# Two of eight low weight parts of a filler job made by an accumulating transfer, and four buffers for the parts

## The chip, the core and the metric

The kernel runs on one core of a Trainium2 chip. The metric is the time of the whole launch on the device, in microseconds. A core has TensorE (PE in the profile; PEld is its weight load), VectorE (DVE), ScalarE (ACT), GpSimd (POOL) and SyncE (SP), each with its own instruction stream, and 16 DMA engines which all of them feed. Here SP issues the loads of the weights, POOL issues small reshuffling transfers and some loads of 256 KB to 512 KB, and ACT issues the stores of results.

## The reference

The reference is one layer of a bidirectional hybrid encoder for a sequence of 256 tokens with 2048 features, in fp32. Cut to what matters here:

```python
mod = silu(c) @ W_ada + b_ada            # shift, scale, gate for mixer and FFN
h = rms_norm(x) * (1 + scale_m) + shift_m
u = h @ W_in                             # q,k,v,o,gates of an mLSTM | q,k,v,z,beta,decay of a gated delta rule | two merge gates
y_a = bidirectional chunkwise mLSTM(u)             @ W_a      # 4 heads
y_b = bidirectional chunkwise gated delta rule(u)  @ W_b      # 16 heads of 128, with a 5-tap convolution
x = x + gate_m * ((g_a * y_a + g_b * y_b) @ W_out)
x = x + gate_f * swiglu(rms_norm(x) * (1 + scale_f) + shift_f)
out = rms_norm(x)
```

The weights of the projections are read once from HBM, and most of TensorE's work is the products of the 256 tokens with them.

## The kernel before

**Products in three parts.** An fp32 product is computed as three products of a shorter type (fp32r in the profile). Each operand is the sum of a high part (the value copied to fp32r) and a low part (the value minus the high part). The result is high times high plus low activation times high weight plus high activation times low weight. The activations are split once (`hh`, `hl` for h). The weights arrive as fp32 and are split on the chip: ScalarE copies a piece of the raw tile to `wh` (line 182 or 213), VectorE subtracts `wh` from the raw piece into `wl` (line 184 or 215).

**Jobs.** A job is one slab of weight columns. `fjob` (line 173) makes 128 columns with the features on the partitions. `tjob` (line 199) makes 512 columns with the tokens on the partitions. The raw weights of a `tjob` come as four chunks `u` of 1 MB, each with four blocks of 128 rows; SP asks for them. Half a chunk, two blocks, is a quantum `(u, k0)` with `k0` 0 or 2, so a job has eight. For each quantum the inner function `halves` (line 207) makes `wh` and `wl`, tiles of 128 x 1024 elements (4 KB for each partition); then come twelve matmuls 128 x 512 (lines 234, 235, 236: high by high, high weight by low activation, low weight by high activation). `wh`, `wl` and the raw tiles are rings of three buffers each; the ring of the raw tiles is shared with the tiles of the modulation weights (`ada`). A part can be written when the matmuls that read the buffer's last content are done.

**Order.** The program is traced in Python as generators that yield after each quantum, and a scheduler may move instructions within what their dependences allow, unless the instruction is wrapped in `order(...)`, which keeps it in program order among the ordered ones of its engine. In `halves` the copy and the subtraction are ordered only where the job makes parts early (`early`). `settle()` runs small pieces of work that were put off; it is called between the copy and the subtraction.

**The delta-rule stage.** From about 131 us to 990 us the kernel computes the delta rule in four groups of four heads: `gdn_phase1` for each head (norms, the products of keys and queries, decays), `gdn_invert` for a group (the inversion of small triangular matrices, VectorE on 64 partitions, with tiles reshuffled by small POOL transfers `inst_d`, `uu`, `inv_d`, `cg`), `gdn_blocks`, and `gdn_phase2` for a pair of heads (chains of small matmuls with VectorE and ScalarE between). These chains leave TensorE time, which filler jobs take: a call of `fill(n)` emits n quanta of the next job. The jobs by token in this stage are z (the delta rule's output gate), v and o (of the mLSTM), mb and ma (the merge gates), four of each; the jobs by feature are the heads' projections `b` and the mLSTM's `a`. VectorE also sums the `ada` tiles in the background (line 111, 128 x 2048).

**After it** come the mLSTM, the branch projections `yb` and `ya`, and the output projection `o` (to about 1240 us), the FFN's gate and up projections `gt`, `up` (to about 1755 us) and its down projection `d`, all with the same `tjob`.

The functions that the diff touches, and what calls them:

Of the kernel before, what the change touches and what calls it, by code (L numbers as in the profile page):

```python
# [10 lines left out]
F32R = mybir.dt.float32r  # L11
AF = mybir.ActivationFunctionType
ALU = mybir.AluOpType
PSUM = bass.MemoryType.PSUM

P = 128
# [36 lines left out]
def hybrid_block(ctx: ExitStack, tc: tile.TileContext, xr, nfr, crow, pk_d, cst_d, ada2, ada4, win0, winb, wint, wba, wbb, wo, wgu, wd, out, dbg=None):  # L53
    nc = tc.nc
    V, S, G, PE = nc.vector, nc.scalar, nc.gpsimd, nc.tensor

    def pool(stack, name, bufs=1, **kw):
        return stack.enter_context(tc.tile_pool(name=name, bufs=bufs, **kw))

    cp = pool(ctx, "cp")  # L60
    st = pool(ctx, "st")
# [9 lines left out]
    def order(ins, yes=True):  # L71

        return tc.keep_in_program_order(ins) if yes else ins
# [62 lines left out]
    def raw_tile(shape, name):  # L136

        since[0] += 1
        if since[0] > 2 and asked and room[0][0] is st:
            add()  # L140
        return st.tile(shape, F32, tag="raw", bufs=3, name=name)
# [4 lines left out]
    def settle(keep=0, only=None):  # L146

        now = [f for f in behind if only is None or f.__name__ == only]
        for f in now[: len(now) - keep]:
            behind.remove(f)  # L150
            f()
# [13 lines left out]
    def pump():  # L165
        count[0] += 1
        if every[0] and count[0] % every[0] == 0:
            owed[0] += 1
        if owed[0] and not held[0]:
            owed[0] -= 1  # L170
            sums()

    def fjob(name, src, done):

        ps = acc_ps.tile([P, 512], F32, tag="acc", name=f"acc_{name}")
        o = ps[:, :T]
        raw = raw_tile([P, KB, P], f"raw_{name}")
        nc.sync.dma_start(raw, src)
        for k0 in range(0, KB, 8):
            wh = st.tile([P, 8, P], F32R, tag="wh", bufs=3, name=f"wh_{name}_{k0}")  # L180
            wl = st.tile([P, 8, P], F32R, tag="wl", bufs=3, name=f"wl_{name}_{k0}")
            S.activation(wh, raw[:, k0 : k0 + 8], AF.Copy)
            settle()
            V.tensor_tensor(wl, raw[:, k0 : k0 + 8], wh.bitcast(F32), ALU.subtract)  # L184
            for k in range(8):
                kk = k0 + k
                PE.matmul(o, wh[:, k], woven(hh[:, kk]), start=kk == 0, stop=False)  # L187
                PE.matmul(o, wh[:, k], woven(hl[:, kk]), start=False, stop=False)  # L188
                PE.matmul(o, wl[:, k], woven(hh[:, kk]), start=False, stop=kk == KB - 1)  # L189
            if k0:  # L190
                pump()
                done(o.rearrange("p (c h) -> p h c", h=2))
            yield True

    def woven(a, n=2):

        return a.rearrange("p (h c) -> p c h", h=n)

    def tjob(name, chunks, xh, xl, done, early=0, by_token=None, steps=1, parts=((0, slice(0, 512)), (1, slice(0, 512)))):

        raws = {}

        def halves(u, k0):
            if u not in raws:
                raws[u] = raw_tile([P, 4, 512], f"raw_{name}_{u}")
                nc.sync.dma_start(raws[u], chunks[u])  # L210
            wh = st.tile([P, 2, 512], F32R, tag="wh", bufs=3, name=f"wh_{name}_{u}_{k0}")
            wl = st.tile([P, 2, 512], F32R, tag="wl", bufs=3, name=f"wl_{name}_{u}_{k0}")
            order(S.activation(wh, raws[u][:, k0 : k0 + 2], AF.Copy), early)  # L213
            settle()
            order(V.tensor_tensor(wl, raws[u][:, k0 : k0 + 2], wh.bitcast(F32), ALU.subtract), early)  # L215
            return wh, wl

        todo = [(u, k0) for u in range(len(chunks)) for k0 in (0, 2)]
        made = []
        for i, q in enumerate(todo[:early]):  # L220
            made.append(halves(*q))
            if steps > 1 or i == early - 1:
                yield True
        ps = [acc_ps.tile([P, 512], F32, tag="acc", name=f"acc_{name}_{t}") for t in range(2)]
        last = 4 * len(chunks) - 1
        if by_token:
            todo = todo[:-2]
        for n, (u, k0) in enumerate(todo):
            wh, wl = made.pop(0) if made else halves(u, k0)
            for k in range(2):  # L230
                kk = 4 * u + k0 + k
                for t in range(2):
                    c = slice(t * P, (t + 1) * P)
                    order(PE.matmul(ps[t], xh[:, kk, c], woven(wh[:, k]), start=kk == 0, stop=False), early and steps > 1)  # L234
                    PE.matmul(ps[t], xl[:, kk, c], woven(wh[:, k]), start=False, stop=False)  # L235
                    PE.matmul(ps[t], xh[:, kk, c], woven(wl[:, k]), start=False, stop=kk == last)  # L236
            if k0:
                pump()
                if u == len(chunks) - 1:
                    done(ps)  # L240
            yield True
            if early and steps > 1:
                if n + early < len(todo):
                    made.append(halves(*todo[n + early]))
                yield True
        if by_token:
            w = [halves(len(chunks) - 1, k0) for k0 in (0, 2)]
            by_token()
            for i, (t, part) in enumerate(parts):
                if i > 1:  # L250
                    ps.append(acc_ps.tile([P, 512], F32, tag="acc", name=f"acc_{name}_{i}"))
                c = slice(t * P, (t + 1) * P)
                o = ps[i][:, : part.stop - part.start]
                for k in range(4):
                    kk = last - 3 + k
                    wh, wl = (woven(a[:, k % 2])[:, part.start // 2 : part.stop // 2] for a in w[k // 2])
                    PE.matmul(o, xh[:, kk, c], wh, start=i == 2 and not k, stop=False)
                    PE.matmul(o, xl[:, kk, c], wh, start=False, stop=False)
                    PE.matmul(o, xh[:, kk, c], wl, start=False, stop=kk == last)
                done(t, ps[i], part)  # L260
                yield True
# [104 lines left out]
    def z_job(g, early=0):  # L366
        def done(ps):
            szs[g] = evp.tile([P, 2, 512], F32, tag="sz", bufs=1, name=f"sz{g}")
            for t in range(2):
                S.activation(szs[g][:, t], ps[t], AF.Silu)  # L370
        return tjob(f"z{g}", [wint[g, u] for u in range(4)], hh, hl, done, early)

    def b_job(h, j):
        return fjob(f"b{h}_{j}", winb[3 * (h - GRP) + j], lambda ps: gdn_conv(h, j, ps))

    def a_qk(h, j):
        return fjob(f"a{h}_{j}", winb[36 + 4 * h + j], keep_f(kq_d[h][j], f"a{h}_{j}"))

    def a_vo(i, h):
        return tjob(  # L380
            f"{'vo'[i]}{h}", [wint[4 + 4 * i + h, u] for u in range(4)], hh, hl,
            keep((v_d, o_d)[i][h], (AF.Copy, AF.Sigmoid)[i], f"{'vo'[i]}{h}"),
        )

    def m_job(i, g):
        return tjob(
            f"m{'ab'[i]}{g}", [wint[12 + 4 * i + g, u] for u in range(4)], hh, hl,
            keep((ma_d, mb_d)[i][g], AF.Sigmoid, f"m{'ab'[i]}{g}"),
        )
# [620 lines left out]
    def invert(g):  # L1010
        gen = gdn_invert(g)
        next(gen)
        fill(4 if g else 6)
        for _ in gen:
            fill(1)

    invert(0)
    for g in range(4):
# [32 lines left out]
        if g < 3:  # L1051
# [3 lines left out]
                add()  # L1055
            invert(g + 1)
    settle()
    sx.close()


# [322 lines left out]
    for j in range(FB // 4):  # L1383
# [4 lines left out]
        for e2 in range(2):  # L1388
            px = gps(f"pxf{j}_{e2}")
            for e in range(2):  # L1390
                f = 2 * e2 + e
# [159 lines left out]
```

## Time and profile before

| | |
|---|---|
| runs of the kernel | 2000.26, 2000.23, 1991.81 us (median 2000.23) |
| the profiled execution | 1994.6 us, span 1992.6 us |
| TensorE busy | 1943.2 us |
| VectorE busy | 1393.9 us |
| ScalarE busy | 1023.7 us |
| POOL busy | 116.8 us |
| read from HBM | 467.07 MB |
| mean granted clock of TensorE | 0.992 |

Busy time counts computing instructions only. In the groups a line reads: line, engine, operation, output and inputs, shape, count, then busy time and mean of one in ns, then the idle time of the engine before them and who ended it. In the list of waits it reads: who waited, for whom, total in us, times, longest. In a timeline it reads: start, duration, engine, line, and in brackets the idle time before it. Matmuls are pipelined, so the durations of neighbours overlap; the distance of their starts is what counts. For a transfer, "to landing" is the time from its issue to its end.

### The profile page before, as it was taken

What the parts mean: (1) busy time and instruction counts of PE and PEld (TensorE: products, weight loads), DVE (VectorE), ACT (ScalarE), POOL (GpSimd) and SP (SyncE); (2) the same over time, 40 slices, a digit from 0 to 9 for tenths busy, and PEclk for the clock granted to TensorE, in tenths of its full rate; (3) what the DMA queues carried; (4) which work ended last, traced back from release to release, by engine and by line L of the source; (5) the groups of instructions that cost most, each with busy time, mean ns of one, the idle gap of its engine ahead of it and who ended that gap; (6) DMA issues with size and microseconds to landing.
All of it is one profiled execution on the core that took longest, in us unless ns stands there. A gap on an engine that the chain in (4) does not pass through costs nothing.

```text
span 1992.6 us, 27027 instructions
## 1 busy us (share of the span) xinstructions
PE 1943.2 (98%) x10386; PEld 1700.4 (85%) x10386; DVE 1393.9 (70%) x2062; ACT 1023.7 (51%) x1541; POOL 116.8 (6%) x211
## 2 busy tenths in 40 slices
PE   8999999999999999999999999999999999999998
PEld 6878789988988899889787888888888888888886
DVE  5778887877878788867576778866666665555554
ACT  3136646765756577655544444554444444444443
POOL 0001210111001101010100000200000000000000
PEclk9999999999989999999999999999999999999999
DMA  9987676655666666587786888466676775555654
GB/s 400 420 336 232 181 245 242 203 183 207 215 197 226 235 235 228 197 283 271 248 300 234 355 298 325 170 252 234 243 263 232 245 262 195 206 199 202 209 195 145
DMA packets 78962, 485.64 MB, mean 244 GB/s; under 512 B 10585, under 2 KB 15969, under 8 KB 24433
## 3 DMA queue, kind: packets, MB, share of 16 engines
q1 hardware_dynamic: 63216, 450.69, 62.4%
q0 software_dynamic: 8160, 17.88, 4.2%
q10 hardware_dynamic: 7458, 15.36, 2.1%
q8 instruction: 81, 1.33, 0.3%
q14 instruction: 47, 0.39, 0.1%
HBM read 467.07 MB, written 16.82 MB: 243 GB/s over the span
## 4 chain that ended last, share of the span: by engine, by line
PE 72%; DVE 12%; DMA 10%; ACT 3%; issue 2%; POOL 0%; ACTq 0%; SPq 0%; DVEq 0%; POOLq 0%
PE acc_gt L234 4%; PE acc_gt L235 4%; PE acc_gt L236 4%; PE acc_up L236 4%; PE acc_up L234 4%; PE acc_up L235 4%; PE acc_d L236 4%; PE acc_d L234 4%; PE acc_d L235 4%; DMA ra<-ada 3%; PE acc_o L236 2%; PE acc_o L234 2%; PE acc_o L235 2%; DMA ada<-ada 2%; PE acc_ya L236 1%
## 5 line engine op out<-in xcount | busy, mean ns | idle before, releaser
L215 DVE TENSOR_TENSOR wl_d<-raw_d,wh_d 128x1024 fp32r<-128x1024 f32 x88 | 107.7, 1224 | 109.2 <-ACT wh_d L213 109.2
L215 DVE TENSOR_TENSOR wl_up<-raw_up,wh_up 128x1024 fp32r<-128x1024 f32 x88 | 107.6, 1224 | 99.9 <-ACT wh_up L213 99.9
L215 DVE TENSOR_TENSOR wl_gt<-raw_gt,wh_gt 128x1024 fp32r<-128x1024 f32 x88 | 108.5, 1233 | 80.0 <-ACT wh_gt L213 80.0
L187 PE MATMUL acc_b<-hh,wh_b 128*128 128x256 f32 x576 | 164.2, 285 | 0.0
L189 PE MATMUL acc_b<-hh,wl_b 128*128 128x256 f32 x576 | 160.2, 278 | 0.1
L188 PE MATMUL acc_b<-hl,wh_b 128*128 128x256 f32 x576 | 159.2, 276 | 0.0
L213 ACT ACTIVATE wh_d<-raw_d 128x1024 fp32r<-128x1024 f32 x88 | 92.9, 1056 | 128.0 <-PE acc_d L235 119.2
L111 DVE SCALAR_TENSOR_TENSOR ada<-ada,crow 128x2048 f32<-128x2048 f32 x64 | 146.2, 2284 | 12.7 <-DMA ada<-ada 12.5
L213 ACT ACTIVATE wh_gt<-raw_gt 128x1024 fp32r<-128x1024 f32 x88 | 92.9, 1056 | 118.6 <-PE acc_gt L235 71.0
L213 ACT ACTIVATE wh_up<-raw_up 128x1024 fp32r<-128x1024 f32 x88 | 92.8, 1055 | 108.1 <-PE acc_up L235 77.1
L234 PE MATMUL acc_gt<-wh_gt,hfh 128*128 128x512 f32 x352 | 135.4, 385 | 0.2 <-ACT hfh L1338 0.2
L235 PE MATMUL acc_gt<-wh_gt,hfl 128*128 128x512 f32 x352 | 134.8, 383 | 0.0
L236 PE MATMUL acc_gt<-wl_gt,hfh 128*128 128x512 f32 x352 | 133.7, 380 | 0.0
L234 PE MATMUL acc_up<-wh_up,hfh 128*128 128x512 f32 x352 | 133.4, 379 | 0.0
L235 PE MATMUL acc_up<-wh_up,hfl 128*128 128x512 f32 x352 | 133.4, 379 | 0.0
L236 PE MATMUL acc_up<-wl_up,hfh 128*128 128x512 f32 x352 | 133.4, 379 | 0.0
L234 PE MATMUL acc_d<-wh_d,ffh 128*128 128x512 f32 x344 | 130.9, 380 | 0.0
L235 PE MATMUL acc_d<-wh_d,ffl 128*128 128x512 f32 x344 | 130.9, 380 | 0.0
L236 PE MATMUL acc_d<-wl_d,ffh 128*128 128x512 f32 x344 | 130.4, 379 | 0.0
L561 PE MATMUL first<-x,raw 128*128 128x256 f32 x512 | 114.5, 382 | 6.9 <-ACT x L555 6.2
L561 PEld LDWEIGHTS first<-x,raw 128*128 128x128 f32 x512 | 96.0, 190 | 25.3 <-ACT x L555 11.8
L189 PEld LDWEIGHTS acc_b<-hh,wl_b 128*128 128x128 f32 x576 | 111.3, 193 | 1.2 <-DVE wl_b L184 1.1
(374 smaller groups left out, 5237.5 us busy)
## 6 DMA issues: line engine op xcount, KB each, us to landing
ada<-ada SPq DMA_DIRECT2D x64, 1024.0 KB, 5.0
raw_gt<-wgu SPq DMA_DIRECT2D x44, 1024.0 KB, 4.9
raw_up<-wgu SPq DMA_DIRECT2D x44, 1024.0 KB, 4.9
raw_d<-wd SPq DMA_DIRECT2D x44, 1024.0 KB, 4.8
raw_b<-winb SPq DMA_DIRECT2D x36, 1024.0 KB, 5.3
ra<-ada SPq DMA_DIRECT2D x32, 1025.0 KB, 15.7
raw<-win SPq DMA_DIRECT2D x16, 1024.0 KB, 14.5
raw_z<-wint SPq DMA_DIRECT2D x16, 1024.0 KB, 5.2
```

Source lines behind the costliest of these rows:

```text
L111: order(V.scalar_tensor_tensor(raw, raw, 1.0, row_c[:, :D], ALU.mult, ALU.mult, accum_out=mod[:, c : c + 1]), room[0][3] > 1)
L187: PE.matmul(o, wh[:, k], woven(hh[:, kk]), start=kk == 0, stop=False)
L188: PE.matmul(o, wh[:, k], woven(hl[:, kk]), start=False, stop=False)
L189: PE.matmul(o, wl[:, k], woven(hh[:, kk]), start=False, stop=kk == KB - 1)
L213: order(S.activation(wh, raws[u][:, k0 : k0 + 2], AF.Copy), early)
L215: order(V.tensor_tensor(wl, raws[u][:, k0 : k0 + 2], wh.bitcast(F32), ALU.subtract), early)
L234: order(PE.matmul(ps[t], xh[:, kk, c], woven(wh[:, k]), start=kk == 0, stop=False), early and steps > 1)
L235: PE.matmul(ps[t], xl[:, kk, c], woven(wh[:, k]), start=False, stop=False)
L236: PE.matmul(ps[t], xh[:, kk, c], woven(wl[:, k]), start=False, stop=kk == last)
L561: PE.matmul(first[o], raw[:, o], x[:, b], start=b == 0 and o % 2 == 0, stop=b == KB - 1 and o % 2 == 1)
```

## The change

The change has four pieces.

1. The rings of `wh` and `wl` have four buffers, in `fjob` and `tjob`, for the whole kernel.
2. In the delta-rule stage, for a job by token that makes no parts early and has no split by token, the quanta at places 3 and 7 of the eight, (1,2) and (3,2), get their low part in another way. ScalarE writes the negated copy of the raw piece to `wl` (rounded to fp32r, it is minus the high part), POOL issues a transfer that reads the same piece of the weights from HBM once more and adds it to `wl`, and ScalarE makes `wh` as before. VectorE has no part in it.
3. These two quanta are made ahead: when quantum n is about to be made and quantum n + 2 is one of them, the parts of n + 2 are made first. Both copies are put in program order. `halves` does not call `settle()` for them.
4. The room for the descriptors of transfers that are built by software is set to 8192, where nothing was given before; the flag `added` is cleared at the end of the stage.

```diff
@@ fjob
-            wh = st.tile([P, 8, P], F32R, tag="wh", bufs=3, name=f"wh_{name}_{k0}")
-            wl = st.tile([P, 8, P], F32R, tag="wl", bufs=3, name=f"wl_{name}_{k0}")
+            wh = st.tile([P, 8, P], F32R, tag="wh", bufs=4, name=f"wh_{name}_{k0}")
+            wl = st.tile([P, 8, P], F32R, tag="wl", bufs=4, name=f"wl_{name}_{k0}")
@@ before tjob
+    added = [True]
+
@@ tjob, halves
-            wh = st.tile([P, 2, 512], F32R, tag="wh", bufs=3, name=f"wh_{name}_{u}_{k0}")
-            wl = st.tile([P, 2, 512], F32R, tag="wl", bufs=3, name=f"wl_{name}_{u}_{k0}")
+            wh = st.tile([P, 2, 512], F32R, tag="wh", bufs=4, name=f"wh_{name}_{u}_{k0}")
+            wl = st.tile([P, 2, 512], F32R, tag="wl", bufs=4, name=f"wl_{name}_{u}_{k0}")
+            if (u, k0) in moved:
+                order(S.activation(wl, raws[u][:, k0 : k0 + 2], AF.Copy, scale=-1.0))
+                G.dma_start(wl, chunks[u][:, k0 : k0 + 2], accum_op=ALU.add)
+                order(S.activation(wh, raws[u][:, k0 : k0 + 2], AF.Copy))
+                return wh, wl
             order(S.activation(wh, raws[u][:, k0 : k0 + 2], AF.Copy), early)
             settle()
             order(V.tensor_tensor(wl, raws[u][:, k0 : k0 + 2], wh.bitcast(F32), ALU.subtract), early)
             return wh, wl
 
         todo = [(u, k0) for u in range(len(chunks)) for k0 in (0, 2)]
+        moved = [] if early or by_token or not added[0] else todo[3::4]
+        sooner = {}
         made = []
...
         for n, (u, k0) in enumerate(todo):
-            wh, wl = made.pop(0) if made else halves(u, k0)
+            if n + 2 < len(todo) and todo[n + 2] in moved:
+                sooner[todo[n + 2]] = halves(*todo[n + 2])
+            wh, wl = made.pop(0) if made else sooner.pop((u, k0)) if (u, k0) in sooner else halves(u, k0)
@@ after the four groups of the delta rule
     settle()
+    added[0] = False
     sx.close()
@@ the program
-    nc = _bacc.Bacc("TRN2", target_bir_lowering=False, num_devices=1)
+    nc = _bacc.Bacc("TRN2", target_bir_lowering=False, num_devices=1, dynamic_dma_scratch_size=8192)
```

## The prediction

> **What bounds the kernel now.** I read the first part of the page (busy time by engine), then the shares of the chain that ended last, then the windows by stage.
>
> ```profile
> span 1992.6 us, 27027 instructions
> PE 1943.2 (98%) x10386; PEld 1700.4 (85%) x10386; DVE 1393.9 (70%) x2062; ACT 1023.7 (51%) x1541; POOL 116.8 (6%) x211
> PE 72%; DVE 12%; DMA 10%; ACT 3%; issue 2%; POOL 0%; ACTq 0%; SPq 0%; DVEq 0%; POOLq 0%
> ```
> ```profile
> core 0: us, PE busy (x) PEld busy (x) DVE busy (x) ACT busy (x) POOL busy (x), PEclk, DMA share, GB/s
> 131.00:900.00 769.00, 743.47 (x4704) 670.21 (x4705) 617.73 (x1196) 493.86 (x870) 93.31 (x178) 0.99 0.67 221
> ```
>
> TensorE is the bound, and the number of its matmuls stays the same. In the delta-rule stage, about 131 to 900 us, it is idle for 769.00 - 743.47 = 25.5 us, while VectorE is busy 80% and ScalarE 64% of the time. Everything that a lighter VectorE can give back lies in those 25.5 us. What ended them is in the waits of TensorE in that window (name, waited for: us in all, times, longest):
>
> ```profile
> PE vps L605 <- ACT vf L341: 6.3, 8, 3.1
> PE acc_mb L236 <- DVE wl_mb L215: 3.1, 3, 1.5
> PE acc_z L234 <- ACT wh_z L213: 2.5, 1, 2.5
> PE acc_z L236 <- DVE wl_z L215: 2.4, 3, 1.5
> PE acc_v L236 <- DVE wl_v L215: 2.4, 3, 1.4
> PE acc_ma L236 <- DVE wl_ma L215: 2.1, 1, 2.1
> PE p L762 <- DVE pt L754: 1.9, 1, 1.9
> PE p L787 <- DVE pt L776: 1.7, 1, 1.7
> PE pa L800 <- DVE UL L736: 1.2, 1, 1.2
> ```
>
> The late low parts make 3.1 + 2.4 + 2.4 + 2.1 = 10.0 us, the delta rule's own VectorE steps 1.9 + 1.7 + 1.2 = 4.8, ScalarE's results 6.3 + 2.5 = 8.8.
>
> ```profile
> 148.41 0.70 PE L236 MATMUL acc_z<-wl_z,hh 128*128 128x512 f32 x2 [1.54 <-DVE wl_z L215]
> ```
> ```profile
> 550.20 1.06 ACT L182 ACTIVATE wh_a<-raw_a 128x1024 fp32r<-128x1024 f32 x1 [4.64 <-DMA raw_a<-winb]
> ```
>
> The last group is partly a matter of transfers: ahead of the 3.1 us wait ScalarE had itself stood 4.64 us for a weight tile. The largest of the z waits, at 148 us, belongs to the first z job, which the change leaves alone.
>
> **The change, part by part.** The prices of the steps, from the groups of instructions and the table of transfers:
>
> ```profile
> L215 DVE TENSOR_TENSOR wl_v<-raw_v,wh_v 128x1024 fp32r<-128x1024 f32 x32 | 38.7, 1215 | 9.6 <-ACT wh_v L213 9.5
> L213 ACT ACTIVATE wh_v<-raw_v 128x1024 fp32r<-128x1024 f32 x32 | 33.7, 1052 | 17.6 <-PE acc_v L235 13.9 <-PE acc_z L235 1.9 <-PE acc_v L236 1.1
> ```
> ```profile
> raw_v<-wint SPq DMA_DIRECT2D x16, 1024.0 KB, 5.2
> mkq<-kq_d POOLq DMA_DIRECT2D x4, 512.0 KB, 7.9
> vt<-v_d POOLq DMA_DIRECT2D x4, 512.0 KB, 9.6
> gtb<-mb_d SPq DMA_DIRECT2D x4, 512.0 KB, 5.0
> sgo<-o_d POOLq DMA_DIRECT2D x4, 512.0 KB, 13.6
> ```
> ```profile
> L934 POOL DMA_DIRECT2D vt<-v_d x4: 531/536/537, 864.4 to 1036.0; - x4
> ```
> ```profile
> L943 POOL DMA_DIRECT2D sgo<-o_d x4: 528/542/549, 975.9 to 998.2; - x4
> ```
>
> Nineteen jobs by token lose two of their eight subtractions (v, mb, o, ma for four groups, z for three): 38 quanta, (1,2) and (3,2) of each.
>
> ```profile
> 653.30 0.40 DVE L696 TENSOR_TENSOR utmp<-uu 64x238 f32<-64x238 f32 x1
> 653.63 1.21 DVE L215 TENSOR_TENSOR wl_ma<-raw_ma,wh_ma 128x1024 fp32r<-128x1024 f32 x1
> ```
>
> *Removed:* 38 subtractions of 1.215 us, 46.2 us of VectorE, 7% of its 617.7. They lie beside TensorE's work; what counts is the 10.0 us of late low parts and the 4.8 us of chain steps. Bounds of the gain: 0 and 25.5. Only a quarter of the subtractions of a job goes, and single late ones remain (the 2.1 us wait ends with the subtraction that starts at 653.63 among the inversion's small steps), but the queue gets shorter for all that follow, and a fourth buffer of each part lets ScalarE and VectorE stand one quantum further ahead. I take 6 of the 10.0 (1.54 of it is out of reach) and 2 of the 4.8: **-8 us**.
>
> *Added on ScalarE:* 38 negating copies of 1.052 us, 40 us in an engine 64% busy. Beside TensorE they cost nothing as long as the next high part is ready. But the program order is kept: at quantum 1 and 5 ScalarE does the negated copy and the high part of the quantum two ahead, then the high part that is needed next, so 3 x 1.06 = 3.2 us instead of 1.06. The cover is TensorE's work between the release of the buffer and the first use. A quantum is 12 matmuls; their pitch is 0.216 us, from the timeline, where the third line follows 0.51 after the second, for a late low part:
>
> ```profile
> 284.51 0.38 PE L234 MATMUL acc_o<-wh_o,hh 128*128 128x512 f32 x1
> 284.73 0.38 PE L235 MATMUL acc_o<-wh_o,hl 128*128 128x512 f32 x1
> 285.24 0.48 PE L236 MATMUL acc_o<-wl_o,hh 128*128 128x512 f32 x1
> ```
>
> Counting matmuls in the changed program's order, a quantum with four buffers mostly has over 5 us, and 3.2 fits. It does not fit where phase steps of the delta rule stand between on ScalarE. The nearest rows are from the third and fourth group:
>
> ```profile
> 811.85 0.48 PE L234 MATMUL acc_z<-wh_z,hh 128*128 128x512 f32 x1 [2.51 <-ACT wh_z L213]
> ...
> 882.15 0.48 PE L236 MATMUL acc_mb<-wl_mb,hh 128*128 128x512 f32 x1 [1.48 <-DVE wl_mb L215]
> ```
> ```profile
> 882.23 1.11 ACT L783 ACTIVATE UL<-p 32x128 f32<-32x128 f32 x4
> 883.37 1.06 ACT L213 ACTIVATE wh_mb<-raw_mb 128x1024 fp32r<-128x1024 f32 x1
> ```
>
> In the last mb job the copies stand behind the four UL copies: 0.4 + 3 x 1.06 = 3.5 against 0.4 of cover, about 3 us where it loses 1.5 now. In the same way I count 2.9 in the second mb job, 3.4 in the first ma, +1.3 in the last z (on top of the 2.51), 1.1 each in the last o and ma, 0.6 in the third z: 3.1 - 1.5 + 2.9 + 3.4 + 1.3 + 2.2 + 0.6 = 12.0; one of these will meet a stall that is there anyway, so **+11**. Bounds: 0 (all hidden) and 38 x 2.1 = 80 (none).
>
> *The transfer:* no accumulating DMA is in the trace. Its chain is copy 1.06, issue 0.53, landing. The copy can start when the buffer's last matmul of four quanta before has ended and must be done after five quanta and two matmuls, 62 x 0.216 = 13.4 us, for 27 of the 38; nine have 5.6 to 12.5, two about 50. So a landing up to 13.4 - 1.6 = 11.8 us is hidden in the common case. Bounds from whole transfers of 512 KB: 5.0 (from SP's queue) and 13.6 (sgo, four close together). Nearest is the same queue, size and direction, alone: 7.9 and 9.6. With 9.6 the chain is 11.2, and the short ones, some lengthened by ScalarE's stalls above, lose 0.5 to 1.9, in sum 4.5 us; with 7.9 it is 0.2. I take **+2**. With 13.6 it would be 27 x 1.8 + 35 for the short ones = 84.
>
> The Trainium skill, "Collectives: The Full Stack", section "The bandwidth ceiling: the fold count and why AG ≠ RS ≠ AR", says of an add in the transfer path that it takes two source reads on one ring and so about half the rate of a copy; no run here shows it yet. By that rule the streaming part, not the fixed part, would double (the rival "late transfer" below has its price).
>
> *POOL:* 38 issues of 0.53 us are 20 us beside 93 busy of 769. Each waits on its copy, and behind it stand the small transfers of the inversion and the alpha loads; delayed by a copy (about 1 us) they cost 0 to 8 (one per inversion and pair), I take 0, since invert steps are covered by filler jobs. If that cover is gone, the next phase's TensorE steps start late.
>
> *More traffic:* 38 x 0.5 = 19 MB on top of 769 us x 221 GB/s = 170 MB: a DMA share of 0.67 x 189 / 170 = 0.75. A load of 1 MB may land later; where VectorE now stands for one it costs at once. Bounds 0 and 38 x 0.5; I take **+1**.
>
> ```profile
> 878.46 2.29 DVE L111 SCALAR_TENSOR_TENSOR ada<-ada,crow 128x2048 f32<-128x2048 f32 x1 [2.04 <-DMA ada<-ada]
> ```
>
> *Four buffers after 900 us, and the halved descriptor room:* in the later stages TensorE has next to no idle time but for start and end, so 0; the room could make POOL's bursts (vt, sgo) wait once for a landing, 0 to 10, I take 0, as the transfers of this stage are 10 us and more apart.
>
> *Sum:* -8 + 11 + 2 + 1 = **+6 us**. Against the profiled execution (1994.6 us, span 1992.6) that is 2000.6; against the runs' median of 2000.23, which has one run of three at 1991.81, it is 2006. I predict between them, 2003.
>
> **The rivals.**
>
> *A, VectorE's relief wins.* ScalarE's extra copies hide, since ScalarE idles 275 us of the stage, and the fourth buffer takes most of the 10.0 + 4.8, and part of the 8.8: -12 to -25, so about 1985 (1975 to 1990). For it: the low parts are the largest group of waits. Against: half of the waits are single events that have another cause.
>
> *C, ScalarE's order wins (slower).* The place is the quantum after a moved one. It decides once the average of the 38 places pays over 0.5 us: with the listed 12.0 kept, nothing gained, and 0.5 us at 20 other places, +22, so about 2022 (2011 to 2035). For it: the 2.51 and the UL rows, where a high part is late already with one copy ahead. Against: cover over 5 us in most places.
>
> *D, late transfer.* It decides at a landing of 11.8 us. A transfer that streams its 512 KB twice adds up to half of raw_v's 5.2 us to vt's 9.6: 12.2, a chain of 13.8, 0.4 x 27 + 23 for the short ones = +34; in place of my 2, 2003 + 32 = 2035. At sgo's 13.6 it is 2085. For it: sgo's median is over the limit. Against: the other three rows are under it by 2 us and more, and so its chance is the smallest. By the rule of the Trainium skill cited above it would be the likely one; no row here can show that.
>
> **How the numbers follow.** Chances: no change 0.35, A 0.27, C 0.21, D 0.17. A measurement here tells about 0.5%, 10 us, from no change, so faster 0.27, same 0.35, slower 0.38. The likeliest case alone ranges from 1991 to 2010; the range that leaves out no more than 2 in 10 runs from 1977 (a gain of 23) to 2060 (a landing of about 13 us).
>
> **What would show it.** Right: VectorE busy about 46 us less, ScalarE 40 more, POOL 38 more issues; the wl waits on VectorE in the window smaller than 10.0 by about 6; new waits of line 234 for wh in mb, ma and z jobs, together about 11 us; landing of the new transfers 7 to 11 us with TensorE waiting for them under 5 us; DMA share 0.75. Wrong: TensorE's waits name the added DMA by tens of us (D), waits on wh all over (C), or idle time under 15 us (A).

## The result, and the profile after

The changed kernel takes 2046.3 us (median, 2043.87 to 2055.76) against 1996.33 us for the kernel before in the same comparison: a ratio of 1.026, 95% interval 1.022 to 1.030. It is slower by about 50 us. The time lies inside the range of the prediction, but 43 us above the predicted 2003, and outside the 1991 to 2010 us of "no change", which was the likeliest case.

The profiled execution of the changed kernel is its slowest, 2055.76 us, so the trace shows some 10 us more than the median. The line numbers of the changed kernel differ: the negated copy is line 216, the transfer 217, the moved high part 218, the other copies and subtractions 220 and 222, the three matmuls 245, 246, 247. First the head of the page and the shares of its chain:

```profile
span 2054.0 us, 27016 instructions
PE 1967.5 (96%) x10386; PEld 1714.4 (83%) x10386; DVE 1352.1 (66%) x2024; ACT 1049.8 (51%) x1578; POOL 153.9 (7%) x249
PE 63%; DMA 15%; DVE 11%; ACT 7%; issue 3%; POOL 0%; ACTq 0%; SPq 0%; DVEq 0%; POOLq 0%
```

The work has moved as described: VectorE is busy 41.8 us less, ScalarE 26.1 us and POOL 37.1 us more (the prediction had 46 and 40 for the first two). But in the chain the share of transfers rose from 10% to 15% and that of ScalarE from 3% to 7%. TensorE's idle time grew from 1992.6 - 1943.2 = 49.4 us to 2054.0 - 1967.5 = 86.5 us. And the same 10386 matmuls were busy for 24.3 us more. The second number is as telling as the first: it is 24.3 of the 61.4 us that the span grew by, and the last section explains it.

The window of the delta-rule stage, which now ends about 50 us later:

```profile
131.00:950.00 819.00, 763.00 (x4681) 680.93 (x4682) 576.77 (x1158) 514.25 (x898) 125.57 (x212) 0.97 0.73 226
```

What TensorE waited for from 131 to 960 us (the largest):

```profile
PE acc_z L245 <- ACT wh_z L220: 11.3, 5, 5.8
PE acc_mb L245 <- ACT wh_mb L220: 7.0, 4, 2.9
PE acc_v L247 <- DVE wl_v L222: 6.5, 2, 6.1
...
PE acc_mb L247 <- DMA wl_mb<-wint: 0.3, 1, 0.3
```

The waits for a high part went from one of 2.5 us to 18.3 us in the first two lines alone. The waits for late low parts of VectorE in the jobs by token, which the change was to shorten, are no shorter: all of them together are 14.9 us here, where they were 10.5 us from 131 to 900 us before. For an accumulating transfer TensorE waited only 0.3 us. The table of transfers says why:

```profile
raw_v<-wint SPq DMA_DIRECT2D x16, 1024.0 KB, 6.7
raw_a<-winb SPq DMA_DIRECT2D x13, 1024.0 KB, 6.8
wl_v<-wint POOLq DMA_DIRECT2D x8, 512.0 KB, 5.8
wl_mb<-wint POOLq DMA_DIRECT2D x8, 512.0 KB, 5.7
vt<-v_d POOLq DMA_DIRECT2D x4, 512.0 KB, 8.1
```

The accumulating transfers land in 5.7 to 5.8 us, sooner than plain 512 KB loads of the same queue (8.1 us here), and far below the 11.8 us at which they would show. The raw loads, though, land later: raw_v 6.7 us in place of 5.2. ScalarE's waits for transfers in the same window:

```profile
ACT wl_mb L216 <- DMA raw_mb<-wint: 27.6, 5, 7.4
ACT wh_b L182 <- DMA raw_b<-winb: 22.0, 10, 7.3
ACT wl_z L216 <- DMA raw_z<-wint: 20.8, 3, 8.2
ACT wl_v L216 <- DMA raw_v<-wint: 20.5, 6, 8.3
ACT wl_o L216 <- DMA raw_o<-wint: 17.0, 6, 5.0
ACT wl_ma L216 <- DMA raw_ma<-wint: 10.9, 2, 6.2
```

The negated copy (line 216) stands for its raw tile 96.8 us in 22 waits. In the kernel before all of ScalarE's waits for raw tiles were 21.4 us from 131 to 1000 us, the largest of them:

```profile
ACT wh_z L213 <- DMA raw_z<-wint: 8.1, 2, 4.8
```

Now they are 141.2. One such place, in the timeline of ScalarE and then of TensorE:

```profile
918.79 1.06 ACT L216 ACTIVATE wl_mb<-raw_mb 128x1024 fp32r<-128x1024 f32 x1 [7.43 <-DMA raw_mb<-wint]
919.75 1.04 ACT L218 ACTIVATE wh_mb<-raw_mb 128x1024 fp32r<-128x1024 f32 x1
920.70 1.04 ACT L220 ACTIVATE wh_mb<-raw_mb 128x1024 fp32r<-128x1024 f32 x1
```
```profile
921.79 0.48 PE L245 MATMUL acc_mb<-wh_mb,hh 128*128 128x512 f32 x1 [2.88 <-ACT wh_mb L220]
```

The copy at 918.79 is not needed for two quanta, but it was put ahead in program order and its raw tile was not there. The copy that TensorE needs next, at 920.70, has its raw tile already and stands behind. So a wait of 7.43 us on something early became a wait of 2.88 us on something due.

### The profile page after: what moved, and what is told of

Read it like the earlier page. It is cut to its first block, busy times and chain, and to the rows that moved or that the text cites. A ratio compares the mean times of both kernels' runs of the same rounds, so it can differ in the third digit from the quotient of the medians.

```text
span 2054.0 us, 27016 instructions
## 1 busy us (share of the span) xinstructions
PE 1967.5 (96%) x10386; PEld 1714.4 (83%) x10386; DVE 1352.1 (66%) x2024; ACT 1049.8 (51%) x1578; POOL 153.9 (7%) x249
## 4 chain that ended last, share of the span: by engine, by line
PE 63%; DMA 15%; DVE 11%; ACT 7%; issue 3%; POOL 0%; ACTq 0%; SPq 0%; DVEq 0%; POOLq 0%
PE acc_gt L245 4%; PE acc_gt L246 4%; PE acc_gt L247 4%; PE acc_up L245 4%; PE acc_up L247 4%; PE acc_up L246 4%; PE acc_d L247 4%; PE acc_d L246 4%; PE acc_d L245 4%; DMA ra<-ada 3%; DMA ada<-ada 3%; PE acc_o L247 2%; PE acc_o L246 2%; PE acc_o L245 2%; DMA raw_mb<-wint 2%
## 5 line engine op out<-in xcount | busy, mean ns | idle before, releaser
L222 DVE TENSOR_TENSOR wl_up<-raw_up,wh_up 128x1024 fp32r<-128x1024 f32 x88 | 107.4, 1225 | 96.8 <-ACT wh_up L220 96.8
L572 PEld LDWEIGHTS first<-x,raw 128*128 128x128 f32 x512 | 96.0, 190 | 25.6 <-ACT x L566 12.3
```

The costliest lines, as they stand in the source:

```text
L572: PE.matmul(first[o], raw[:, o], x[:, b], start=b == 0 and o % 2 == 0, stop=b == KB - 1 and o % 2 == 1)
```

## The experiments

All times are medians; the kernel before stood at 1992 to 1994 us beside them. Four theories were held against each other: (1) the wait for the raw tile at copies made ahead, (2) the two extra copies in ScalarE's order, whatever they wait for, (3) the added traffic, (4) the buffers and the smaller descriptor room.

**Four buffers alone.**

```diff
-        moved = [] if early or by_token or not added[0] else todo[3::4]
+        moved = []
```

> Four buffers of the parts and the smaller descriptor room alone; no quantum is moved. Theory 1 (the negated copy, made two quanta ahead and kept in program order, asks for the next raw tile a quantum earlier than before; ScalarE stands for it, 96.8 us in 22 waits, with the next high part behind it), theory 2 (two more copies in ScalarE's order, whatever they wait for) and theory 3 (the added traffic makes the raw loads late) all expect the time of before or a little less, 1985 to 2000 us. Theory 4 (the buffers or the room change the order or the queues for the worse) expects 2015 or more.

Measured: 2000.0 us, ratio 1.003 (1.0015 to 1.0045). The buffers and the room bring nothing; they cost some 6 us. Theory 4 carries a small part. The waits say what the buffers did. TensorE's waits for late low parts of these jobs fell from 10.5 us to 3.0 in the profiled run, so the buffers alone took more from these waits than the 6 us that the prediction hoped to take. But the waits for the delta rule's own VectorE steps (`pt`, `UL`, `R` and `r`) rose from 6.2 us to 16.8, the largest of them:

```profile
PE p L773 <- DVE pt L765: 7.1, 2, 4.9
```

Why they rose is not shown.

**The relief by itself.** The 38 quanta have no low part, the high part is read in its place; nothing is made ahead.

```diff
             if (u, k0) in moved:
-                order(S.activation(wl, raws[u][:, k0 : k0 + 2], AF.Copy, scale=-1.0))
-                G.dma_start(wl, chunks[u][:, k0 : k0 + 2], accum_op=ALU.add)
-                order(S.activation(wh, raws[u][:, k0 : k0 + 2], AF.Copy))
-                return wh, wl
+                S.activation(wh, raws[u][:, k0 : k0 + 2], AF.Copy)
+                settle()
+                return wh, wh
```

> Four buffers, nothing made ahead, and the 38 quanta have no low part of their own: the matmuls read the high part in its place, so VectorE does 38 subtractions less and nothing is added on ScalarE, POOL or the queues; the low part's product is left out. It measures the gain term of the prediction by itself against the run with four buffers alone (2000). The term was 8 us: 1988 to 1995. If VectorE's load doesn't set the end: 1996 to 2004.

Measured: 1995.06 us, 5 us below the run with four buffers alone, and a ratio of 1.001 (0.999 to 1.003) to the kernel before. The two intervals, of this run and of the four buffers alone, overlap, so the 5 us are near the noise. The 38 quanta also take no buffer from the ring of `wl` here. This is about what the change could gain at most with these buffers: 38 subtractions taken away for nothing make the kernel no faster than it was. TensorE's largest waits there are no longer low parts but the delta rule's own VectorE steps:

```profile
PE pa L809 <- DVE UL L745: 6.3, 3, 3.6
PE p L771 <- DVE pt L763: 5.1, 2, 4.8
```

**Made ahead, but split as all others.**

```diff
-                order(S.activation(wl, raws[u][:, k0 : k0 + 2], AF.Copy, scale=-1.0))
-                G.dma_start(wl, chunks[u][:, k0 : k0 + 2], accum_op=ALU.add)
                 order(S.activation(wh, raws[u][:, k0 : k0 + 2], AF.Copy))
+                V.tensor_tensor(wl, raws[u][:, k0 : k0 + 2], wh.bitcast(F32), ALU.subtract)
                 return wh, wl
```

> The same 38 quanta are made two ahead, but split as all others: one ordered copy on ScalarE, the subtraction on VectorE; no negated copy and no transfer. Theory 1: the ordered copy stands for the raw tile just as the negated one did, so 2030 to 2055 us, and over 70 us of ScalarE's waits for raw tiles. Theory 2: one extra copy ahead instead of two, so about half of the loss, 2015 to 2030. Theory 3: no added traffic, so 1990 to 2005.

Measured: 2015.65 us, ratio 1.012 (1.009 to 1.014). Making the quanta ahead in program order costs 16 us over the run with four buffers, with no further copy and no transfer. (The edit also skips `settle()` for these 38 quanta, as the change does; no run takes the two apart.) ScalarE waits 93.6 us for raw tiles in it (12.3 us with four buffers alone), the largest at copies made ahead:

```profile
ACT wh_o L216 <- DMA raw_o<-wint: 20.9, 6, 5.3
```

The waits were as theory 1 expected, the time was not: it is a part of the loss, not the whole.

**No transfer.**

```diff
-                G.dma_start(wl, chunks[u][:, k0 : k0 + 2], accum_op=ALU.add)
```

> The changed kernel without the accumulating transfers; the negated copy alone stays in the low part, which is so the negated high part and not the remainder: the work of the transfer is left out. Theory 1 and theory 2: 2030 to 2050 us, since ScalarE's order and its waits stay. Theory 3: the raw loads land as before (5.2 us) and the time falls to 1990 to 2010.

Measured: 2027.97 us, ratio 1.018 (1.016 to 1.019). The transfers account for 18 of the 50 us. This lies between what the theories expected.

**The transfer cut to a sixteenth.**

```diff
-                G.dma_start(wl, chunks[u][:, k0 : k0 + 2], accum_op=ALU.add)
+                G.dma_start(wl[:, 0, :128], chunks[u][:, k0, :128], accum_op=ALU.add)
```

> The changed kernel with each accumulating transfer cut to a sixteenth, 128 of the columns of one block in place of 1024 elements of each partition; the rest of the low part stays the negated high part, so most of the remainder is left out. The issues, their place on POOL's queue and their waits stay, the 19 MB of traffic go. If the 18 us between the run without transfers (2028) and the changed kernel (2046) come from the bytes (raw loads that land later): 2026 to 2034. If they come from the queue and the wait for the landing: 2040 to 2050.

Measured: 2026.73 us, ratio 1.017 (1.014 to 1.019), the same as with no transfer. So the 38 issues and their place on POOL's queue cost nothing here; the bytes do. (The small transfers also land sooner, at 2.7 to 3.3 us; for those of full size TensorE waited the 0.3 us shown above.) The raw loads land sooner again (raw_a 6.8 us in the changed kernel), and ScalarE's waits for them fall from 141.2 to 107.4 us:

```profile
raw_a<-winb SPq DMA_DIRECT2D x13, 1024.0 KB, 4.9
```

The sum of these waits is not a price, though: with no transfer at all it was 83.5 us, and the kernel took the same time.

**One quantum ahead instead of two.**

```diff
-            if n + 2 < len(todo) and todo[n + 2] in moved:
-                sooner[todo[n + 2]] = halves(*todo[n + 2])
+            if n + 1 < len(todo) and todo[n + 1] in moved:
+                sooner[todo[n + 1]] = halves(*todo[n + 1])
```

> The changed kernel with the moved quanta made one ahead instead of two: the raw tile is then asked for at the same quantum as before, and the same 38 negated copies, transfers and buffers stay. Theory 1: ScalarE's waits for raw tiles at the negated copy fall from 96.8 us to under 40 and the time to 1990 to 2015 us; the transfer (copy 1.06, issue 0.93, landing 5.8) still fits. Theory 2 and theory 3: the loss stays, 2035 to 2050.

Measured: 2057.99 us, ratio 1.032 (1.030 to 1.034), slower than the change. ScalarE's waits for raw tiles did go, to 23.4 us in all (5.8 at the negated copies). But now TensorE waited for the transfers and still for high parts:

```profile
PE acc_v L245 <- ACT wh_v L220: 7.2, 3, 6.0
PE acc_o L247 <- DMA wl_o<-wint: 6.3, 3, 3.5
...
PE acc_v L247 <- DMA wl_v<-wint: 5.5, 4, 4.1
```

The expectation of theory 1 was wrong here, since the edit also took one quantum of cover from the transfer. Two ahead is what hides the transfer, and one ahead is what keeps ScalarE from standing for the raw tile; none of the runs with three raw tiles has both.

**The raw supply: three buffers of the parts, and then a fourth raw tile in the room they leave.**

```diff
-            wh = st.tile([P, 2, 512], F32R, tag="wh", bufs=4, name=f"wh_{name}_{u}_{k0}")
-            wl = st.tile([P, 2, 512], F32R, tag="wl", bufs=4, name=f"wl_{name}_{u}_{k0}")
+            wh = st.tile([P, 2, 512], F32R, tag="wh", bufs=3, name=f"wh_{name}_{u}_{k0}")
+            wl = st.tile([P, 2, 512], F32R, tag="wl", bufs=3, name=f"wl_{name}_{u}_{k0}")
```

(the same two lines in `fjob`), and for the second run also, wherever the ring is named,

```diff
-        return st.tile(shape, F32, tag="raw", bufs=3, name=name)
+        return st.tile(shape, F32, tag="raw", bufs=4, name=name)
```

> The changed kernel with three buffers of each part as before, all else as in the change. It is the partner of the next run. If the fourth buffer helps the moved quanta (the copy could then start four quanta before the use and not three): slower than the changed kernel, 2055 to 2080 us. If the buffer works only as in the run with four buffers alone, which was 6 us slower than before: 2036 to 2046.

> As the run with three buffers of each part, and the room that this leaves is given to a fourth raw tile, so that a raw tile can be asked for earlier. Theory 1 (ScalarE stands for the raw tile at the copies made ahead): its waits for raw tiles fall to under 40 us and the time by 20 us or more against the partner. Theory 2 (the extra copies themselves) and theory 3 (the traffic): within 8 us of the partner.

Measured: 2064.6 us (1.034, 1.031 to 1.038) with three raw tiles, 2032.86 us (1.020, 1.017 to 1.023) with four. So the fourth buffer of the parts, which cost 6 us alone, is worth 18 us once quanta are moved (2064.6 to 2046.3). The fourth raw tile wins 32 us, and ScalarE's waits for raw tiles from 131 to 1000 us go from 86.8 us to the one line that is left:

```profile
ACT wh_b L182 <- DMA raw_b<-winb: 3.8, 1, 3.8
```

**Four raw tiles with no quantum moved**, the partner of that run (the edit of the first experiment on top).

> Four raw tiles, three buffers of each part, the smaller descriptor room, and no quantum moved: the kernel before with one more raw tile. It is the partner of the run with four raw tiles in which the quanta are moved (2033). Theory 1 (the raw supply is the main term): that run loses against this one only by traffic and the copies, so this one comes out at 1985 to 1996 us, at or under the kernel before, which stands 21.4 us for raw tiles. If the raw supply never ended a wait of TensorE before: 1993 to 2002.

Measured: 1994.31 us, ratio 1.0004 (0.9989 to 1.0019). The fourth raw tile is worth nothing without the moved quanta. So the shortage is made by the change, and 32 us of loss hung on it where the parts have three buffers. This kernel is the nearest to a better version that was found, and it is no better. It has the smaller descriptor room too, which thus costs nothing that the fourth raw tile doesn't give back.

**Four raw tiles, the quanta moved, the small transfer.**

> Four raw tiles, three buffers of each part, the 38 quanta moved, and the transfer cut to a sixteenth (most of the remainder is left out). With the raw wait and the bytes both gone, what is left against the run without moved quanta is the two extra copies in ScalarE's order and the wait for a short landing. Theory 1 with theory 3: 1995 to 2010 us. Theory 2: 2020 or more.

Measured: 2014.71 us, ratio 1.010 (1.007 to 1.013). With the raw wait and the bytes gone, 20 us of loss are left against the partner without moved quanta, more than theories 1 and 3 allow and less than theory 2 had. The waits for high parts come to only 5.4 us in it (none in the partner). The bytes cost 2032.86 - 2014.71 = 18 us here too, but by another way: with the raw tiles in time, TensorE waited 17.3 us for three late transfers in the run with the full ones, and 6.7 us for one in this one. The first two lines are of the run with the full transfers, the last three of this one:

```profile
PE acc_mb L247 <- DMA wl_mb<-wint: 10.5, 2, 6.5
...
PE acc_v L247 <- DMA wl_v<-wint: 6.8, 1, 6.8
```
```profile
254.49 0.52 POOL L673 DMA_DIRECT2D uu<-inst_d  x1 [6.00 <-DMA inst_d<-mi]
...
255.78 0.98 POOL L217 DMA_DIRECT2D wl_v<-wint  x1
```
```profile
266.64 0.80 PE L247 MATMUL acc_v<-wl_v,hh 128*128 128x512 f32 x1 [6.67 <-DMA wl_v<-wint]
```

This wait of 6.7 us is no matter of bytes: it stands at the same place in both runs. The negated copy was done at 250.27 us, but POOL stood 6.00 us for a small transfer of the inversion and issued this one only at 255.78, and its 64 KB then landed 10.8 us later, where the median is 2.8. So the transfer's place among POOL's other transfers does cost here, where the raw tiles are in time.

**The quantum's own high part first, then the copies of the one two ahead.**

```diff
+            wh, wl = made.pop(0) if made else sooner.pop((u, k0)) if (u, k0) in sooner else halves(u, k0)
             if n + 2 < len(todo) and todo[n + 2] in moved:
                 sooner[todo[n + 2]] = halves(*todo[n + 2])
-            wh, wl = made.pop(0) if made else sooner.pop((u, k0)) if (u, k0) in sooner else halves(u, k0)
```

> The changed kernel with the moved quantum's copies behind the quantum's own high part instead of ahead of it, still two quanta ahead: ScalarE may stand as long for the raw tile, but the part that TensorE needs next is made by then. If what is behind the waiting copy is what costs: 2005 to 2025 us. If ScalarE's wait also holds up the delta rule's own steps: 2030 to 2046.

Measured: 2035.91 us, ratio 1.022 (1.019 to 1.026). Only 10 us of the loss go. ScalarE's waits for raw tiles fall from 141.2 to 47.1 us, 9.7 of them at the negated copy. The quantum's own high part is no longer behind, but the next quantum's now is, and a high part is still what TensorE waits for longest (8.2 us at 256.42 us, where ScalarE had itself stood 5.26 us for a step of VectorE ahead of the copies). The time lies in the second range that was expected, but the reason given there isn't the one that the waits show. The transfers also start later and land later (medians 6.5 to 7.8 us), and TensorE waits for them about 9 us in its three largest such lines.

```profile
PE acc_v L245 <- ACT wh_v L220: 9.0, 2, 8.2
```

**One moved quantum per job instead of two.**

```diff
-        moved = [] if early or by_token or not added[0] else todo[3::4]
+        moved = [] if early or by_token or not added[0] else todo[7::8]
```

> The changed kernel with one moved quantum per job, the last one (3,2), in place of two: 19 negated copies and 19 transfers. If every moved quantum costs about the same on top of the four buffers (2000 us; 46 us for 38): 2020 to 2026 us. If single places carry the loss and the later quantum isn't among them, as with the first of the v jobs, where the largest wait lies: 2000 to 2012. If it beats the kernel before, under 1990, the loss is a matter of dose.

Measured: 2026.37 us, ratio 1.016 (1.013 to 1.019). Half the dose costs 26 of the 46 us over four buffers, which is 1.2 to 1.4 us for each moved quantum on average, and at neither of the two doses did the gain come out ahead.

## Why the prediction was right or wrong

One chain of runs leads from the kernel before to the changed one (the steps depend on the order in which they are taken): four buffers 1994 to 2000, +6; made ahead in program order 2000 to 2015.7, +16; a negated copy in place of the subtraction 2015.7 to 2028, +12; the transfer 2028 to 2046.3, +18. Together +52. The prediction had +6. That its range held the time is luck: its upper end, 2060, was set for a transfer that lands after about 13 us, and the transfers landed after 5.8.

- *The bound and the room* held: TensorE sets the time, and a lighter VectorE had little to give.
- *VectorE's relief, -8*: the term counted the fourth buffer as a help and took 6 us from the late low parts. The waits for low parts did fall by more than that, with the buffers alone, but the waits for the delta rule's own steps grew by as much, and the buffers came out at +6. The relief is then -5 against four buffers alone, near the noise, and both together are +1 (0.999 to 1.003) against the kernel before. Waits that go were counted as time that goes. Rival A falls with this.
- *ScalarE's copies, +11*: the mechanism was seen, the size was not. The negated copies in place of the subtractions cost 12 us in the chain above. With raw tiles in time and almost no bytes, 20 us are left net of the relief, of which the profile shows 5.4 as waits for high parts and 6.7 as the late small transfer. The place in the last z job of the changed kernel shows the mechanism:

```profile
854.47 1.06 ACT L216 ACTIVATE wl_z<-raw_z 128x1024 fp32r<-128x1024 f32 x1
855.43 1.04 ACT L218 ACTIVATE wh_z<-raw_z 128x1024 fp32r<-128x1024 f32 x1
856.37 2.93 ACT L220 ACTIVATE wh_z<-raw_z 128x1024 fp32r<-128x1024 f32 x3
```
```profile
857.47 0.80 PE L245 MATMUL acc_z<-wh_z,hh 128*128 128x512 f32 x1 [5.84 <-ACT wh_z L220]
```

  Two copies that nobody needs yet stand ahead of three, the first of which is due. The prediction put +1.3 on top of the 2.51 us there; it was +3.3.
- *What was left out*: that the copies made ahead would also wait. The prediction counted the copies' durations in ScalarE's order, and their release by the buffer, but not their other operand. The first half of chunk 1 or 3 is due one quantum after the place where the change reads its second half, and a ring of three raw tiles, refilled just in time, does not have it yet. This is the step that failed: "made two quanta ahead" was priced as 3 x 1.06 us and not as a wait for a 1 MB load. The 141.2 us of waits, the 16 us of the run made ahead by VectorE and the 32 us of the fourth raw tile show it. That ScalarE's wait then costs as much as it does goes by what stands behind it, and not by the sum of the waits.
- *More traffic, +1*: measured +18. The DMA share came out near the computed one (0.73 for 0.75), in a window that is 50 us longer. What was wrong is the step from a later landing to the time. In the changed kernel the median raw load lands 0.1 to 1.5 us later than in the run without transfers, and ScalarE was already standing for raw tiles. That these later landings make the 18 us is argued and not shown: with four raw tiles the bytes cost 18 us as well, with hardly a wait for raw tiles, and 10.5 us of them as a wait for two late transfers. The term's own bound, 38 x 0.5 = 19, held it; the value was taken at the wrong end.
- *The transfer, +2*: right in mechanism and better in size. The landing is 5.7 to 5.8 us and hidden in the change; rival D's landing did not come. About half of the landing is not streaming: 64 KB with the add took 2.7 to 3.3 us. But a byte that is added in this way did take the DMA engines about twice as long as a loaded one. POOL's queue before and after, and the queue of the weight loads after (packets, MB, share of the 16 engines' span):

```profile
q0 software_dynamic: 8160, 17.88, 4.2%
```
```profile
q1 hardware_dynamic: 63216, 450.69, 59.5%
q0 software_dynamic: 13632, 37.80, 9.6%
```

  The 19.92 MB more on q0 took 9.6% of 2054.0 us less 4.2% of 1992.6, which is 113.5 us or 5.7 us for each MB; the loads of q1 took 2.7. Packet by packet in the trace: 4864 packets of 4 KB are new on this queue, most took 320 to 340 ns and hardly any less, while more than half of the queue's plain packets of 4 KB took 150 to 165 ns in the kernel before. Eight of the new packets for each of 16 engines make an estimate of 2.6 us for the streaming of one transfer, about the difference between 64 KB and 512 KB. This agrees with the rule of the Trainium skill ("Collectives: The Full Stack", section "The bandwidth ceiling: the fold count and why AG ≠ RS ≠ AR") of a halved rate for an add. So the rule held for the packets, and the landing of rival D did not follow from it, as 9.6 us of a plain load was the wrong base for it. The prediction counted the traffic at the rate of a plain load.
- *POOL, 0*: right in the changed kernel; a sixteenth of the bytes with all issues costs the same as no issues (2026.73 and 2027.97 us). With four raw tiles it was not: the transfer that stood behind the inversion's made TensorE wait 6.7 us. One issue took 0.93 us, not 0.53.
- *The rivals*: C was priced at 2022 with only ScalarE's durations. Its place was right, the quantum after a moved one, and what stands in front of it was more than copies. Of the chances, no change at 0.35 was the largest single case, and the result was none of the four as described: C's place, with the raw wait and with traffic on top.

What stays open is how the 20 us of the run with four raw tiles and the small transfer divide between the two copies, their place in the order and the one late small transfer of 6.7 us, and why the waits moved to the delta rule's own steps with four buffers. The runs don't tell these apart.

## What to carry to other kernels

A step that is made ahead and kept in program order makes its engine wait for all that the step reads: price the arrival of each operand at the new place, not only the duration of the instruction. Added bytes can cost even when the added transfer itself is hidden: here 18 us with 0.3 us of waits for it. Before work is moved off an engine, take it away for nothing and time that: here the whole gain was about 5 us, and nothing against the kernel before. A wait that a change removes may come back at the next step of the same engine.

## What the runs showed of the hardware

A wait of TensorE can cost more than its length. After the 6.12 us wait at 180.74 us (VectorE had stood 6.34 us for an alpha load), the matmuls are slower:

```profile
174.25 0.38 PE L246 MATMUL acc_v<-wh_v,hl 128*128 128x512 f32 x1
180.74 0.79 PE L247 MATMUL acc_v<-wl_v,hh 128*128 128x512 f32 x1 [6.12 <-DVE wl_v L222]
181.33 0.63 PE L245 MATMUL acc_v<-wh_v,hh 128*128 128x512 f32 x1
181.76 0.63 PE L246 MATMUL acc_v<-wh_v,hl 128*128 128x512 f32 x1
...
185.17 0.52 PE L245 MATMUL acc_v<-wh_v,hh 128*128 128x512 f32 x1
185.52 0.38 PE L246 MATMUL acc_v<-wh_v,hl 128*128 128x512 f32 x1
```

From 181.33 to 185.17 us the distance from start to start is 0.43 us, twice the 0.216, and the granted clock in the stretch from 180 to 183 us is 0.50. From 180.74 to 185.52 eleven distances take 4.78 us instead of 2.38, so 2.4 us come on top of the 6. Over the run the granted clock fell from 0.992 to 0.983, and the same matmuls were busy 24.3 us longer. The stretches at half the clock (without the end of the run) are 3.4 or 6.8 us long; there are 5 in the kernel before, 24 us in all, and 15 in the changed one, 65 us. Half of the 41 us between them is 20.5, which is most of the 24.3. The prediction had priced every wait at its length.

The Trainium skill, "TensorE: Matmul & The Clock Gate", Part 1, gives about 3.4 us of idle as the window after which the clock halves; the 6.12 us wait agrees, and so do the slower matmuls after the 5.84 us wait above. But shorter waits close together can do it too. Around the wait of 2.88 us that ends at 921.79 TensorE was busy 0.70 us in a stretch of 3.40, and the next 3.40 us were at half the clock (the last three numbers are the granted clock, the DMA share and GB/s):

```profile
919.30:922.70 3.40, 0.70 (x2) 0.30 (x2) 0.93 (x1) 3.38 (x6) 0.88 (x1) 1.00 1.01 327
922.70:926.10 3.40, 3.05 (x7) 2.51 (x8) 0.29 (x1) 3.33 (x6) 0.00 (x0) 0.50 1.04 269
```

How busy TensorE must be in such a stretch to keep its clock is not shown.
